# Hybrid decoder trunk: a sum of squares as a row product, a scan's products one piece later, and a second state buffer in linear attention

## The chip, the cores and the metric

The kernel runs on one core of a Trainium2 chip. The metric is the device time of one execution in microseconds (us). The kernel before took 2375.83 us (median of three runs, 2368.9 to 2376.44).

The core's engines have short names in the views: PE (TensorE's matmuls) and PEld (its weight loads), DVE (VectorE), ACT (ScalarE), POOL (GpSimd) and SP (SyncE, which here only issues DMAs). Each engine works through its own queue in order. DMAs are issued from SP's and from ACT's queue.

## What is computed

One layer of a decoder over 2048 tokens and 16 learned meta tokens, width 1024. A combined projection of the normed input feeds two branches: a Mamba-2 state-space branch (16 heads in 4 groups) and gated linear attention (4 heads). The branches are gated, projected, merged, projected once more and normed. The change touches two places of it, cut here to what matters:

```python
# state-space branch: after the scan, an RMS norm over each group's 256 channels
y = jnp.concatenate([y_m, y_r], axis=1) + d_skip[:, None] * xs
y = y.reshape(b, l, D_SSD) * jax.nn.silu(z)
y_ssd = rmsnorm(y.reshape(b, l, SSD_GROUPS, D_SSD // SSD_GROUPS),
                ssd_norm_w.reshape(SSD_GROUPS, -1)).reshape(b, l, D_SSD)

# linear attention: the state that goes from chunk to chunk
def step(s, inp):
    qi, ki, vi, gi = inp
    o_inter = jnp.einsum('bhtk,bhkv->bhtv', qi * jnp.exp(gi), s)
    ...
    g_last = gi[:, :, -1]
    k_dec = ki * jnp.exp(g_last[:, :, None, :] - gi)
    s_new = jnp.exp(g_last)[..., None] * s + jnp.einsum('bhsk,bhsv->bhkv', k_dec, vi)
    return s_new, o_inter + o_intra
```

## The kernel before

**Tiling and stages.** The tokens are worked through in four blocks of 512 (the first also holds the 16 meta tokens). In a block, features lie on the 128 partitions and tokens along the free dimension. Most products are split: each fp32 operand is cut into a high and a low part (fp32r), and `accum` (L187) makes three matmuls of them, high by high, high by low, low by high. A projection of one tile of 128 features (`proj_feat`, L193) is 8 x 3 = 24 matmuls with 512 columns. After the four blocks comes a second stage with the gates, the branch products and the output product, which the change doesn't touch.

**The order of the work.** The main loop (L850 to L860) runs over blocks, and in each block over 4 state-space groups (`ssd_proj`, L475) and 4 attention heads (`gla_proj`, L675). Both are generators. From one yield to the next they emit one projection; this is called a *piece* here. A state-space group has 6 pieces: four feature tiles (two of x, one each of B and C), then two tiles of the gate z. Group 0 has two more ahead of them, for the first values and the time steps. After each piece `step()` (L835) moves every running side generator on to its next yield, the oldest first. Such generators are the scan of a group (`ssd_scan`, begun at the fourth feature tile, L501), the scan of a head (`gla_scan`, begun after the keys, L644), the gates' logarithms (`gates`, L428), the loading of the next block's input (`fetch_u`), and `make_sums` (L73), which loads pieces of earlier results through SP, subtracts them on POOL (L81) and stores them through ACT's queue (L84). For PE and SP the order in which the program emits instructions is the order in which they run (the manual schedule of L849). For DVE, ACT and POOL a scheduler decides the order when the program is built, with its own estimate of times.

**Accesses and buffers.** The framework puts in the semaphores. Tiles come from pools with a number of buffers per tag: "act" (pairs of feature tiles, 4), "tok4" (6), "sq" (5), "gg" (4), "c1" (6), and for PSUM "pj" and "pt" (3 banks each) and "pc" (2 banks). A new tile waits until a buffer of its tag is free.

**The state-space scan** (`ssd_scan`, L518). Its first part fetches a row of cumulated decays (`fetch_cb`) and the factors `yf` by DMA. The part after the next yield makes the first products on PE: the scores of all four chunks (L551), then transposes of the first chunk (L565); they read the feature tiles that ACT (L497) and DVE (L498) finish. Then come four chunks of 128 tokens, one a part. The tail adds the skip term and multiplies by the gate (L613, L615), squares on ACT (L616) and adds the two tiles (L617) into `zs[0]`. One piece later PE sums over the channels: four matmuls (L621) with a strided quarter of `zs[0]` as the stationary operand and a column of ones as the moving one give the sums of 512 tokens as a [128, 4] tile. `rstd_of` (L230) takes the reciprocal root: DVE (L232), then POOL (L233). The result goes to DRAM (L623) and comes back broadcast over the partitions (L625). Two pieces later L630 on DVE multiplies and L631 stores the branch's result.

**The attention scan** (`gla_scan`, L685). After seven levels of products between halves of chunks (L734) and the assembly of the scores, the four chunks are done two to a piece. In each chunk one PSUM bank `po` takes two products: `po[:, 256:]` the state's increment (three matmuls on `kdt`), `po[:, :256]` the output (three on `atp`, and then L808, query times old state, in fp32). DVE then makes the new state in place:

```python
accum(po[:, 256:], [t[:, c] for t in kdt], vc, True, True)
accum(po[:, :256], [t[:, c] for t in atp], vc, True, False)
nc.tensor.matmul(po[:, :256], q[:, c * P:(c + 1) * P], s_gla[:, h], start=False, stop=True)
nc.vector.scalar_tensor_tensor(s_gla[:, h], s_gla[:, h], egl[:, c:c + 1], po[:, 256:],
                               op0=ALU.mult, op1=ALU.add)
```

These are L806 to L810. L811 and L813 on ACT copy the output out of `po` and square it.

**Other names.** `dt_chain` (L377) computes the time steps of a block; its results `tkd`, `tkc`, `wde`, `dec` have two buffers each (L365), and it uses scratch tiles `de`, `dw`, `dl`. The row of 512 sums or roots per group goes through small DRAM tiles (L368).

Of the kernel before, what the change touches and what calls it, by code (L numbers as in the profile page):

```python
# [7 lines left out]
F32 = mybir.dt.float32  # L8
# [6 lines left out]
P = 128  # L15
# [10 lines left out]
NSQ = 5  # L26
NT4 = 6
NACT = 4
NC1 = 6
LEVELS = (1, 2, 4, 8, 16, 32, 64)  # L30
NMSK = len(LEVELS)
# [10 lines left out]
def trunk_kernel(ctx: ExitStack, tc: tile.TileContext, xm, xmt, w_feat, w_tok, w_vm, w_br, w_o,  # L42
# [311 lines left out]
    def new_block(b, u):  # L354
        o = Block()
        o.b, o.u = b, u
        o.m0 = META if b == 0 else 0
        o.tt = o.m0 + BLK
        o.segs_all = [(0, o.tt // 2), (o.tt // 2, o.tt // 2)] if b == 0 else [(0, BLK)]
        o.segs_real = [(o.m0, BLK)]  # L360
        o.starts = [o.m0 + c * P for c in range(NCH)]
        o.chunks = ([(0, META)] if o.m0 else []) + [(a, P) for a in o.starts]
        o.ci0 = 1 if o.m0 else 0
        o.nck = len(o.chunks)
        for nm in ("tkd", "tkc", "wde", "dec"):  # L365
            setattr(o, nm, mk(bpool, [P, 5, NH], F32, nm, bufs=2))
        o.cumd = mk(dpool, [NH, BLK], F32, "cumd")
        o.ecud = mk(dpool, [NH, BLK], F32, "ecud")  # L368
        o.rstd = [mk(dpool, [P, NCH], F32, f"rstd{g}") for g in range(SG)]
        o.g_all = mk(bpool, [P, GH, META + BLK], F32, "g_all")  # L370
        o.gla = {}
        o.alr = mk(bpool, [P, 5, 48], F32, "alr")
        o.mov = lambda kt, a, n: tuple(t[:, kt, a:a + n] for t in u)
        return o


    def dt_chain(o, psd):  # L377
        m0, nck, ci0 = o.m0, o.nck, o.ci0
        tkd, tkc, wde, dec = o.tkd, o.tkc, o.wde, o.dec

        def t80(tag):
            return mk(sm, [P, 5, NH], F32, tag, bufs=1)[:, :nck]

        x = t80("dx")
        for i in range(nck):
            nc.vector.tensor_tensor(x[:, i], psd[i][:, 256:272], hv[:, 0], op=ALU.add)
            nc.scalar.activation(
                o.alr[:, i].rearrange("p (r c) -> p r c", c=16),
                psd[i][:, 272:288].unsqueeze(1).to_broadcast([P, 3, 16]), AF.Copy)
        e = t80("de")  # L390
        nc.scalar.activation(e, x, AF.Abs)
        nc.scalar.activation(e, e, AF.Exp, scale=-1.0)
        w1 = t80("dw")
        nc.vector.tensor_scalar(w1, e, 1.0, None, op0=ALU.add)
        ln = t80("dl")
        nc.scalar.activation(ln, w1, AF.Ln)
        nc.vector.scalar_tensor_tensor(e, w1, 1.0, e, op0=ALU.subtract, op1=ALU.subtract)
        nc.vector.tensor_tensor(ln, ln, e, op=ALU.subtract)
        dt = tkd[:, :nck]
        nc.vector.scalar_tensor_tensor(dt, x, 0.0, ln, op0=ALU.max, op1=ALU.add)  # L400
        nc.vector.tensor_tensor(x, dt, nega.unsqueeze(1).to_broadcast([P, nck, NH]), op=ALU.mult)
        yield
        ps = bank(pt, "pt")
        nc.tensor.matmul(ps[:, :nck * NH], tri, x.rearrange("p c h -> p (c h)"), start=True, stop=True)
        nc.vector.tensor_copy(tkc[:, :nck].rearrange("p c h -> p (c h)"), ps[:, :nck * NH])
        ps = bank(pt, "pt")
        if m0:
            nc.tensor.matmul(ps[:, :NH], ones[:META], x[:META, 0], start=True, stop=True)
        nc.tensor.matmul(ps[:, ci0 * NH:nck * NH], ones, x[:, ci0:].rearrange("p c h -> p (c h)"),
                         start=True, stop=True)  # L410
        psv = ps[:, :nck * NH].rearrange("p (c h) -> p c h", h=NH)
        nc.scalar.activation(dec[:, :nck], psv, AF.Exp)
        nc.vector.tensor_tensor(wde[:, :nck], psv, tkc[:, :nck], op=ALU.subtract)
        nc.vector.tensor_scalar(wde[:, :nck], wde[:, :nck], 0.0, None, op0=ALU.min)
        nc.scalar.activation(wde[:, :nck], wde[:, :nck], AF.Exp)
        nc.vector.tensor_tensor(wde[:, :nck], wde[:, :nck], dt, op=ALU.mult)
        yield
        ps = bank(pt, "pt")
        for c in range(NCH):
            nc.tensor.transpose(ps[:NH, c * P:(c + 1) * P], tkc[:, ci0 + c], ident)  # L420
        cr = mk(wk, [P, 3 + META + BLK], F32, "cin")[:NH, :BLK]
        nc.scalar.activation(cr, ps[:NH], AF.Copy)
        nc.scalar.dma_start(o.cumd, cr)
        er = mk(wk, [P, 3 + META + BLK], F32, "cin")[:NH, :BLK]
        nc.scalar.activation(er, ps[:NH], AF.Exp)
        nc.scalar.dma_start(o.ecud, er)
# [48 lines left out]
    def ssd_proj(o, g):  # L475
        m0, tt = o.m0, o.tt
        feats, zs = [], []
        if g == 0:
            yield from first_values(o)
        for j in range(4):  # L480
            ti = g * 4 + j
            pss = proj_feat(f"s{ti}", w_feat[T_SSD + ti], o.segs_all, o.mov)
            cin = mk(wk, [P, 3 + META + BLK], F32, "cin")
            acc = mk(wk, [P, META + BLK], F32, "acc")[:, :tt]
            nc.scalar.activation(cin[:, 0:3], tails[:, ti, :], AF.Copy)
            for ps, (a, n) in zip(pss, o.segs_all):
                nc.scalar.activation(cin[:, 3 + a:3 + a + n], ps[:, :n], AF.Copy)
                nc.scalar.activation(acc[:, a:a + n], ps[:, :n], AF.Identity, scale=hcw[:, ti, 3:4],  # L488
                                     bias=hcb[:, ti:ti + 1])
            nc.gpsimd.tensor_copy(tails[:, ti, :], cin[:, tt:tt + 3])  # L490
            for k in range(3):
                nc.vector.scalar_tensor_tensor(acc, cin[:, k:k + tt], hcw[:, ti, k:k + 1], acc,  # L492
                                               op0=ALU.mult, op1=ALU.add)
            if j % 2 == 0:
                two = pair_tile()
            f = two[:, j % 2]
            nc.scalar.activation(f[:, :tt], acc, AF.Tanh)  # L497
            nc.vector.scalar_tensor_tensor(f[:, :tt], f[:, :tt], 1.0, acc, op0=ALU.add, op1=ALU.mult)  # L498
            feats.append(f)
            if j == 3:  # L500
                begin(ssd_scan(o, g, feats, zs))  # L501
            yield
        for j in range(2):
            ti = 2 * g + j
            ps, = proj_feat(f"z{ti}", w_feat[T_Z + ti], o.segs_real, o.mov)
            zt = mk(wk, [P, BLK], F32, "gg", bufs=4)
            nc.scalar.activation(zt, ps, AF.Tanh, scale=0.5)
            nc.vector.scalar_tensor_tensor(zt, zt, 1.0, ps, op0=ALU.add, op1=ALU.mult)
            zs.append(zt)
            yield  # L510
# [7 lines left out]
    def ssd_scan(o, g, feats, zs):  # L518
# [4 lines left out]
        yf = mk(wk, [P, NCH, 256], F32, "tok4", bufs=NT4).rearrange("p c f -> p (c f)").rearrange("p (j t) -> p j t", j=2)  # L523
        for i in range(2):
            nc.scalar.dma_start(yf[64 * i:64 * i + 64], o.ecud[4 * g + i:4 * g + i + 3:2, :].unsqueeze(0).to_broadcast([64, 2, BLK]))
        yield
        hs = slice(4 * g, 4 * g + 4)

# [87 lines left out]
            nc.scalar.activation(zs[j], yf[:, j], AF.Square)  # L616
        nc.vector.tensor_tensor(zs[0], zs[0], zs[1], op=ALU.add)  # L617
        yield
        ps = bank(pt, "pt")
        for c in range(NCH):  # L620
            nc.tensor.matmul(ps[:, c:c + 1], zs[0][:, c::NCH], ones[:, :1], start=True, stop=True)  # L621
        r = rstd_of(ps[:, :NCH], NCH, 1.0 / 1024)
        nc.scalar.dma_start(o.rstd[g], r)  # L623
        rb = mk(wk, [P, BLK], F32, "gg", bufs=4)
        nc.scalar.dma_start(rb, o.rstd[g].rearrange("p c -> (p c)").unsqueeze(0).to_broadcast([P, BLK]))  # L625
        yield
        yield
# [37 lines left out]
    def gla_out_gates(o, h):  # L665
        t0 = T_GLA + 4 * h
        for j in range(2):
            ps, = proj_feat(f"g{t0 + 2 + j}", w_feat[t0 + 2 + j], o.segs_real, o.mov)
            gg = mk(wk, [P, BLK], F32, "gg", bufs=4)
            nc.scalar.activation(gg, ps, AF.Tanh, scale=0.5)  # L670
            nc.vector.scalar_tensor_tensor(gg, gg, 1.0, ps, op0=ALU.add, op1=ALU.mult)
            o.gla[h][1].append(gg)
            yield
# [11 lines left out]
    def gla_scan(o, h, kq, vals, gs):  # L685
# [111 lines left out]
        split(*[t[:, 2:] for t in atp], ps[:, :256].rearrange("p (c t) -> p c t", t=P))  # L797
        yield

        vt = vals[0]  # L800
        ot = mk(wk, [P, NCH, 256], F32, "ot", bufs=1)
        ssq = mk(sm, [P, 4], F32, "ssq")
        for c in range(NCH):
# [1 line left out]
            vc = [t[:, c] for t in vt]  # L805
            accum(po[:, 256:], [t[:, c] for t in kdt], vc, True, True)  # L806
            accum(po[:, :256], [t[:, c] for t in atp], vc, True, False)
            nc.tensor.matmul(po[:, :256], q[:, c * P:(c + 1) * P], s_gla[:, h], start=False, stop=True)  # L808
            nc.vector.scalar_tensor_tensor(s_gla[:, h], s_gla[:, h], egl[:, c:c + 1], po[:, 256:],
                                           op0=ALU.mult, op1=ALU.add)  # L810
            nc.scalar.activation(ot[:, c], po[:, :256], AF.Copy)  # L811
            jk = mk(wk, [P, 256], BF16, "junk", bufs=1)
            nc.scalar.activation(jk, po[:, :256], AF.Square, accum_out=ssq[:, c:c + 1])  # L813
# [426 lines left out]
```

## Time and profile before

| | us |
|---|---|
| median of three runs | 2375.83 |
| lowest and highest | 2368.9, 2376.44 |
| the profiled execution | 2377.53 |
| its span, first to last instruction | 2375.7 |
| blocks 0 to 3 with both branches, in the span | 0 to about 1577 |
| second stage, in the span | about 1577 to 2375.7 |

The mean granted TensorE clock of the profiled execution was 0.979 of the full one. PE's busy time by the windows of the profile was 244.6 us of the first 272 us, 174.1 of the next 178 (up to 450), and 775.3 of the 798.7 us of the second stage.

How to read it: the views name a group of instructions by its line in the kernel, its engine, its operation and its tiles (out<-in, with the buffer numbers left out). `L189` to `L191` are the three matmuls of `accum`; the tiles tell which product it is. `L237` and `L238` are the two halves of `split`. A wait is idle time of an engine ahead of an instruction, with the instruction or the DMA that ended it. An idle engine costs time only where PE later waits for it.

### The profile page before, as it was taken

The page shows a single profiled execution, that of the slowest core. Times are in us where ns is not written, and L with a number is a line of the kernel's source. Part 1 is how long each engine was busy: PE and PEld are TensorE (multiplying, and loading weights), DVE is VectorE, ACT ScalarE, POOL GpSimd, SP SyncE. Part 2 cuts the span into 40 slices and gives each one's busy share as a digit, 9 for nine tenths or more (in the row PEclk, how much of TensorE's full clock was granted, in tenths as well). Part 3 has the DMA queues.
Part 4 walks back from the last instruction along what each step waited for, and adds up shares of the span by engine and source line. Part 5 has one row for each costly group of instructions (what it writes and reads, how often), then busy time and mean ns, then how long its engine had stood idle before and what let it go on. Part 6 is the DMA issues. An engine that isn't in the chain of part 4 may idle for free.

```text
span 2375.7 us, 34516 instructions
## 1 busy us (share of the span) xinstructions
PE 2270.2 (96%) x12009; PEld 1925.5 (81%) x12009; DVE 1445.9 (61%) x2467; ACT 1091.8 (46%) x2390; POOL 679.7 (29%) x681
## 2 busy tenths in 40 slices
PE   7999999999999999999999999979999999999998
PEld 6888888877888887888887789867888888888776
DVE  5676664466654456555356554455578854778776
ACT  4655554454433354433345333354545454554443
POOL 4343432212211112221112200027433355424231
PEclk9999999999999999999999999989999999999999
DMA  8776875777776677786587754457667876687743
GB/s 294 250 233 226 268 244 187 224 220 238 243 257 184 206 238 226 222 269 214 179 246 214 226 165 155 142 166 246 208 243 262 285 243 213 237 278 262 249 147 125
DMA packets 310877, 530.66 MB, mean 223 GB/s; under 512 B 30832, under 2 KB 146800, under 8 KB 310704
## 3 DMA queue, kind: packets, MB, share of 16 engines
q1 hardware_dynamic: 200400, 402.84, 52.6%
q10 hardware_dynamic: 110304, 125.63, 16.5%
q8 instruction: 94, 1.54, 0.3%
q14 instruction: 79, 0.65, 0.1%
HBM read 381.00 MB, written 147.36 MB: 222 GB/s over the span
## 4 chain that ended last, share of the span: by engine, by line
PE 71%; DMA 11%; DVE 6%; issue 4%; ACT 4%; POOL 2%; SPq 1%; ACTq 1%; POOLq 0%; DVEq 0%
PE pj L189 16%; PE pj L191 16%; PE pj L190 16%; PE pt L189 3%; PE pt L191 3%; PE pt L190 3%; PE pt L734 2%; DVE acc L492 2%; PE pc L190 2%; PE pc L189 2%; PE pc L191 2%; POOL wr L81 2%; DMA gg<-rstd 2%; DMA wr<-y 1%; PE pc L590 1%
## 5 line engine op out<-in xcount | busy, mean ns | idle before, releaser
L189 PE MATMUL pj<-u,whl 128*128 128x512 f32 (+1 forms) x1440 | 554.5, 385 | 6.1 <-ACT acc L488 3.9
L191 PE MATMUL pj<-u,whl 128*128 128x512 f32 (+1 forms) x1440 | 533.4, 370 | 0.8 <-POOL whl L170 0.8
L190 PE MATMUL pj<-u,whl 128*128 128x512 f32 (+1 forms) x1440 | 533.1, 370 | 0.0
L189 PEld LDWEIGHTS pj<-u,whl 128*128 128x128 f32 x1440 | 275.9, 192 | 52.5 <-ACT acc L488 5.6
L191 PEld LDWEIGHTS pj<-u,whl 128*128 128x128 f32 x1440 | 274.3, 190 | 47.7 <-POOL whl L170 1.1
L190 PEld LDWEIGHTS pj<-u,whl 128*128 128x128 f32 x1440 | 275.7, 191 | 42.4
L189 PE MATMUL pj<-b,a 128*128 128x512 f32 x640 | 254.5, 398 | 10.1 <-ACT sn L952 8.0
L190 PE MATMUL pj<-b,a 128*128 128x512 f32 x640 | 252.1, 394 | 1.8 <-DVE b L911 1.8
L191 PE MATMUL pj<-b,a 128*128 128x512 f32 x640 | 252.6, 395 | 0.0
L170 POOL TENSOR_TENSOR whl<-wr,whl 128x512 fp32r<-128x512 f32 (+1 forms) x100 | 133.4, 1339 | 191.1 <-ACT whl L169 168.5
L911 DVE TENSOR_TENSOR b<-br,b 128x512 fp32r<-128x512 f32 x196 | 152.7, 799 | 47.7 <-ACT b L910 45.2
L492 DVE SCALAR_TENSOR_TENSOR acc<-cin,hcw,acc 128x512 f32<-128x512 f32 (+1 forms) x192 | 159.9, 833 | 34.3 <-ACT acc L488 33.1
L926 POOL TENSOR_TENSOR as<-ar,ar 128x512 f32<-128x512 f32 x40 | 60.5, 1512 | 409.1 <-DMA ar<-in_w_br 151.0
L910 ACT ACTIVATE b<-br 128x512 fp32r<-128x512 f32 x196 | 119.2, 626 | 103.6 <-DMA br<-br_t 32.3
L936 DVE TENSOR_TENSOR a<-ar,a 128x512 fp32r<-128x512 f32 x160 | 126.8, 800 | 65.6 <-ACT a L935 63.5
L81 POOL TENSOR_TENSOR wr<-wr 128x256 f32<-128x256 f32 x80 | 69.0, 862 | 338.1 <-DMA wr<-y 142.6
L189 PEld LDWEIGHTS pj<-b,a 128*128 128x128 f32 x640 | 121.5, 190 | 38.5 <-ACT sn L952 10.2
L189 PE MATMUL pj<-whl,u 128*128 128x256 f32 (+1 forms) x480 | 143.7, 299 | 2.9 <-ACT u L307 1.5
L190 PEld LDWEIGHTS pj<-b,a 128*128 128x128 f32 x640 | 121.6, 190 | 29.0 <-DVE b L911 2.2
L191 PEld LDWEIGHTS pj<-b,a 128*128 128x128 f32 x640 | 121.5, 190 | 27.7
L191 PE MATMUL pj<-whl,u 128*128 128x256 f32 (+1 forms) x480 | 140.0, 292 | 1.4 <-DVE u L309 1.4
L190 PE MATMUL pj<-whl,u 128*128 128x256 f32 (+1 forms) x480 | 139.7, 291 | 0.0
(270 smaller groups left out, 4738.2 us busy)
## 6 DMA issues: line engine op xcount, KB each, us to landing
whl<-k_s SPq DMA_DIRECT2D x96, 512.0 KB, 4.5
whl<-k_g SPq DMA_DIRECT2D x96, 512.0 KB, 4.3
whl<-k_z SPq DMA_DIRECT2D x48, 512.0 KB, 3.7
wr<-in_w_feat SPq DMA_DIRECT2D x80, 256.0 KB, 4.2
whl<-k_v SPq DMA_DIRECT2D x36, 512.0 KB, 3.8
k_s<-whl SPq DMA_DIRECT2D x32, 512.0 KB, 3.5
cb<-cumd ACTq DMA_DIRECT2D x64, 256.0 KB, 5.4
k_g<-whl SPq DMA_DIRECT2D x32, 512.0 KB, 3.8
```

The costliest lines, as they stand in the source:

```text
L81: nc.gpsimd.tensor_tensor(o, x, y, op=ALU.subtract)
L170: nc.gpsimd.tensor_tensor(hl[:, 1], raw, hl[:, 0].bitcast(F32), op=ALU.subtract)
L189: nc.tensor.matmul(ps, sh, mh, start=first, stop=False, **kw)
L190: nc.tensor.matmul(ps, sh, ml, start=False, stop=False, **kw)
L191: nc.tensor.matmul(ps, sl, mh, start=False, stop=last, **kw)
L492: nc.vector.scalar_tensor_tensor(acc, cin[:, k:k + tt], hcw[:, ti, k:k + 1], acc, op0=ALU.mult, op1=ALU.add)
L590: nc.tensor.matmul(py[:, (2 + j) * P:(3 + j) * P], s_ssd[:, g, j * P:(j + 1) * P], cf[:, a:a + P], start=True, stop=True)
L734: nc.tensor.matmul(ps[:, r * P:(r + 1) * P], packed[0][:, r * P:(r + 1) * P], odd_even(half, m0 + (r + 2) * P, P // (2 * half), k_to_q - 2 ...
L910: nc.scalar.activation(t[:, 0], raw, AF.Copy)
L911: nc.vector.tensor_tensor(t[:, 1], raw, t[:, 0].bitcast(F32), op=ALU.subtract)
L926: nc.gpsimd.tensor_tensor(s1, a21, a22, op=ALU.add)
L936: nc.vector.tensor_tensor(t[:, 1], src, t[:, 0].bitcast(F32), op=ALU.subtract)
```

## The change

The diff, without the lines that only replace a number by a name:

```diff
+NGG = 5
...
         for nm in ("tkd", "tkc", "wde", "dec"):
-            setattr(o, nm, mk(bpool, [P, 5, NH], F32, nm, bufs=2))
+            setattr(o, nm, mk(bpool, [P, 5, NH], F32, nm))
...
+        o.ssq = [mk(dpool, [P, NCH], F32, f"ssq{g}") for g in range(SG)]
...
-        e = t80("de")
+        e = wde[:, :nck]
...
-        w1 = t80("dw")
+        w1 = tkc[:, :nck]
...
-        ln = t80("dl")
+        ln = dec[:, :nck]
...
             nc.scalar.dma_start(yf[64 * i:64 * i + 64], o.ecud[...])
         yield
+        yield
         hs = slice(4 * g, 4 * g + 4)
...
         nc.vector.tensor_tensor(zs[0], zs[0], zs[1], op=ALU.add)
         yield
+        sqh, sql = [mk(wk, [P, BLK], F32R, "sq", bufs=NSQ) for _ in range(2)]
+        nc.scalar.activation(sqh, zs[0], AF.Copy)
+        nc.gpsimd.tensor_tensor(sql, zs[0], sqh.bitcast(F32), op=ALU.subtract)
+        yield
         ps = bank(pt, "pt")
-        for c in range(NCH):
-            nc.tensor.matmul(ps[:, c:c + 1], zs[0][:, c::NCH], ones[:, :1], start=True, stop=True)
-        r = rstd_of(ps[:, :NCH], NCH, 1.0 / 1024)
+        for i, t in enumerate((sqh, sql)):
+            nc.tensor.matmul(ps[:1], ones_r[:, :1], t, start=i == 0, stop=i == 1)
+        rb = mk(wk, [P, BLK], F32, "gg", bufs=NGG)
+        nc.scalar.activation(rb[:1], ps[:1], AF.Copy)
+        nc.scalar.dma_start(o.ssq[g].rearrange("p c -> (p c)").unsqueeze(0), rb[:1])
+        s4 = mk(sm, [P, NCH], F32, "ssq")
+        nc.scalar.dma_start(s4, o.ssq[g])
+        yield
+        r = rstd_of(s4, NCH, 1.0 / 1024)
         nc.scalar.dma_start(o.rstd[g], r)
-        rb = mk(wk, [P, BLK], F32, "gg", bufs=4)
         nc.scalar.dma_start(rb, o.rstd[g].rearrange("p c -> (p c)").unsqueeze(0).to_broadcast([P, BLK]))
...
-        vt = vals[0]
+        vt, s_in = vals[0], s_gla[:, h]
...
-            nc.tensor.matmul(po[:, :256], q[:, c * P:(c + 1) * P], s_gla[:, h], start=False, stop=True)
-            nc.vector.scalar_tensor_tensor(s_gla[:, h], s_gla[:, h], egl[:, c:c + 1], po[:, 256:],
-                                           op0=ALU.mult, op1=ALU.add)
+            s_out = s_gla[:, h] if c % 2 else mk(wk, [P, 256], F32, "c1", bufs=NC1)
+            nc.vector.scalar_tensor_tensor(s_out, s_in, egl[:, c:c + 1], po[:, 256:], op0=ALU.mult, op1=ALU.add)
+            nc.tensor.matmul(po[:, :256], q[:, c * P:(c + 1) * P], s_in, start=False, stop=True)
+            s_in = s_out
```

The parts in words:

- The tail of the state-space scan cuts its summed squares into a high part (ACT) and a low part (POOL), a piece later makes the sum as a row with two matmuls (a column of ones stationary, 512 tokens moving), copies the row out of PSUM, sends it to DRAM and reads it back as [128, 4], and a piece after that takes the root as before. These are two yields more.
- One more yield after the scan's first part moves all the rest of the scan one piece later. The last step of a scan so comes three pieces later than before.
- In the attention scan the first chunk of a piece writes its new state into a "c1" buffer, the second chunk writes it back to `s_gla`. The state's update is emitted ahead of the product of the query and the old state.
- "gg" has five buffers instead of four. `tkd`, `tkc`, `wde` and `dec` have one buffer instead of two, and three of them also serve as scratch in place of `de`, `dw` and `dl`.

More of the change, by code (lines that the diff above doesn't have):

```diff
@@ L505, in ssd_proj @@
             ps, = proj_feat(f"z{ti}", w_feat[T_Z + ti], o.segs_real, o.mov)
-            zt = mk(wk, [P, BLK], F32, "gg", bufs=4)
+            zt = mk(wk, [P, BLK], F32, "gg", bufs=NGG)
             nc.scalar.activation(zt, ps, AF.Tanh, scale=0.5)
@@ L668, in gla_out_gates @@
             ps, = proj_feat(f"g{t0 + 2 + j}", w_feat[t0 + 2 + j], o.segs_real, o.mov)
-            gg = mk(wk, [P, BLK], F32, "gg", bufs=4)
+            gg = mk(wk, [P, BLK], F32, "gg", bufs=NGG)
             nc.scalar.activation(gg, ps, AF.Tanh, scale=0.5)
```

## The prediction

> **What bounds the kernel now.** I read the busy row and the chain of the page, then the view of waits, then the groups by line and short timelines around the lines that the change touches.
>
> ```profile
> span 2375.7 us, 34516 instructions
> PE 2270.2 (96%) x12009; PEld 1925.5 (81%) x12009; DVE 1445.9 (61%) x2467; ACT 1091.8 (46%) x2390; POOL 679.7 (29%) x681
> PE 71%; DMA 11%; DVE 6%; issue 4%; ACT 4%; POOL 2%; SPq 1%; ACTq 1%; POOLq 0%; DVEq 0%
> ```
>
> TensorE (PE) is the bound: it is idle for 2375.7 - 2270.2 = 105.5 us, and its order is written out by hand, so a matmul that waits holds up all that stand behind it. Time can change in three ways only: PE gets less work, a PE wait goes, or a PE wait appears. Work on the other engines costs nothing until PE waits for it. So the waits come next.
>
> ```profile
> POOL wr L81 <- DMA wr<-y: 143.0, 19, 22.0
> ...
> DVE tok L630 <- DMA gg<-rstd: 58.5, 16, 6.1
> ...
> ACT ot L811 <- DVE s_gla L809: 39.3, 48, 1.3
> ...
> DVE s_gla L809 <- PE pc L808: 33.2, 32, 5.6
> ...
> PE pc L808 <- DVE s_gla L809: 16.6, 10, 2.5
> ...
> PE pc L551 <- DVE act L498: 11.0, 7, 2.5
> PE pt L621 <- DVE gg L617: 10.7, 6, 3.5
> ```
>
> The columns are total us, times, longest us. The last three rows are PE's own and each belongs to one part of the change: the attention state (L808), the scan's first products (L551), the sum of squares (L621). The other rows matter for what is queued where.
>
> **The row product.** Each of the 16 scans has four fp32 matmuls of one column, which the trace shows as eight instructions.
>
> ```profile
> L621 PE MATMUL pt<-ones_r,gg 128*128 128x1 f32 x128 | 30.3, 358 | 10.7 <-DVE gg L617 10.7
> ...
> L779 PE MATMUL pt<-sq,ones_r 128*128 128x512 f32 x32 | 11.8, 453 | 0.0
> ```
>
> ```profile
> 615.23 1.80 PE L621 MATMUL pt<-ones_r,gg 128*128 128x1 f32 x8
> 616.89 1.14 PE L551 MATMUL pc<-act 128*128 128x128 f32 x8
> ```
>
> From the first of the eight to the next work is 616.89 - 615.23 = 1.66 us. The new form, two matmuls of 512 columns with a stationary of ones, stands in this kernel already: L779, 16 pairs. The groups give the difference: 30.3 - 11.8 = 18.5 us less PE work. The 10.7 us of waiting before L621 goes as well, since the products are emitted two pieces behind the addition L617 instead of one, and a piece is a projection of 24 matmuls, some 9 us (24 x 370 ns). The new ACT copy and POOL subtraction fit into that piece, by these rows of the same shapes:
>
> ```profile
> L237 ACT ACTIVATE sq<-sq 128x512 fp32r<-128x512 f32 x16 | 10.0, 622 | 8.2 <-DVE tok L630 8.1 <-DVE c L742 0.2
> ...
> L170 POOL TENSOR_TENSOR whl<-wr,whl 128x512 fp32r<-128x512 f32 (+1 forms) x100 | 133.4, 1339 | 191.1 <-ACT whl L169 168.5 <-PE pt L757 6.5 <-PE pt L191 6.1
> ```
>
> That is 0.62 + 1.34 = 1.96 us of 9. If the cover is gone (POOL stuck behind L81, third rival), PE pays.
>
> **The scan's first products a piece later.** The 11.0 us of L551 waiting for the feature tiles (L498) goes, since they get 9 us more and the longest wait is 2.5 us. The scan now spans 12 pieces instead of 9 before its last step. What that holds longer: yf (6 "tok4" buffers: at most three yf and two values at once in the SSD groups), the feature pairs (4 "act" buffers: in group 1, with the gates' own pair, the third feature tile waits a piece longer for its buffer, and its products also come a piece later, so the slack stays), the "sq" buffers (two halves, one mask, two decay tiles: all five) and the "gg" buffers (five, so the fifth is needed). I cost all of these at nothing; the cover is the added piece, and without it they are L551 waits again, 11.0 us at most. The single buffers of tkd, tkc, wde, dec, and their use as scratch, cost nothing: the next block writes them 20 pieces after the last scan read them.
>
> **The two added DMAs.** The sum goes to DRAM as a row and comes back as four columns, both on ACT's queue, before L232. Their nearest rows are those of the reciprocal root:
>
> ```profile
> L623 ACTq DMA_DIRECT2D rstd<-rstd x16: 322/336/344, 138.7 to 1423.3; - x16
> L625 ACTq DMA_DIRECT2D gg<-rstd x16: 326/338/357, 142.6 to 1424.8; - x16
> ...
> DMA to landing us min/median/max: 1.4/4.8/7.0
> ```
>
> So ACT issues 2 x 0.34 us more a scan and its queue stands for up to a landing (4.8 us) at the second DMA, which waits for the first; behind it stand the PSUM evictions of the projection. L232 on VectorE (DVE) now waits for a landing too; DVE already stands 58.5 / 16 = 3.7 us at L630 for the same reason. PE's share of such standing cannot be read off directly. Lower bound 0 (everything that stands catches up before PE needs it), upper bound 16 us, one us for each of the 16 scans, about a quarter of DVE's existing 3.7 us. I take 6 us, nearer the lower end, since PE waits for an eviction (ACT acc L488) are a few us in the whole of the existing kernel:
>
> ```profile
> L189 PE MATMUL pj<-u,whl 128*128 128x512 f32 (+1 forms) x1440 | 554.5, 385 | 6.1 <-ACT acc L488 3.9
> ```
>
> Scan part: -18.5 - 10.7 - 11.0 + 6 = -34 us. Bounds: -40 (nothing given back) and -20 (14 us more given back: 10 us of the 21.7 us of waits reappear behind busy DVE and ACT, and 10 us of standing).
>
> **The second state buffer.** It frees the update L809 from the read of the old state by L808. But the update is now also emitted ahead of L808, and both use one PSUM bank: `po[:, 256:]` is read, `po[:, :256]` is written. The trace shows what a shared bank means here. L811 reads only `po[:, :256]`, L809 only `po[:, 256:]`; they share no data, yet ACT waited for L809 48 times of 64 (39.3 us, above). A clean pair of chunks, PE, then DVE, then ACT:
>
> ```profile
> 361.14 0.28 PE L191 MATMUL pc<-tok,atp 128*128 128x256 f32 x1
> 361.25 0.59 PE L808 MATMUL pc<-s_gla,act 128*128 128x256 f32 x2
> ...
> 362.27 0.28 PE L191 MATMUL pc<-tok,atp 128*128 128x256 f32 x1
> 362.51 0.70 PE L808 MATMUL pc<-s_gla,act 128*128 128x256 f32 x2
> ```
>
> ```profile
> 361.98 0.47 DVE L809 SCALAR_TENSOR_TENSOR s_gla<-s_gla,egl,pc 128x256 f32<-128x256 f32 x1
> 363.25 0.48 DVE L809 SCALAR_TENSOR_TENSOR s_gla<-s_gla,egl,pc 128x256 f32<-128x256 f32 x1 [0.79 <-PE pc L808]
> ```
>
> ```profile
> 362.49 0.38 ACT L811 ACTIVATE ot<-pc 128x256 f32<-128x256 f32 x1 [0.63 <-DVE s_gla L809]
> 363.76 0.38 ACT L811 ACTIVATE ot<-pc 128x256 f32<-128x256 f32 x1 [0.53 <-DVE s_gla L809]
> ```
>
> L808 of the second chunk ended at 362.51 + 0.70 = 363.21; both L809 and L811 could have started, L809 ran 363.25 to 363.73, and L811 began only at 363.76. So accesses to one bank by two engines are put in program order, even reads of different halves. A write by PE after a read by DVE will be too. The Trainium skill, "PSUM — Partial Sum Buffer", section "PSUM bank collisions raise a hardware error", gives this rule: two engines at one bank and the same partitions at once collide, disjoint columns included, so the order must be guarded by bank and not by address. By that rule the wait below appears, without it the first rival comes out; the ACT rows agree, and no run here yet shows a PE write held up by a DVE read.
>
> New order in one chunk: six matmuls, then L809, then L808. From the rows: the sixth ends at 361.14 + 0.28 = 361.42; L809 starts 0.04 later (363.21 to 363.25), takes 0.48, and PE follows 0.06 after it (361.98 + 0.47 = 362.45, L808 at 362.51). L808 starts at 362.00 instead of 361.25: 0.75 us, in each of 64 chunks: 48 us. Before, only the second chunk of a pair could wait, and most of its wait lay beside its own six matmuls.
>
> The 16.6 us of existing waits come from DVE being busy or itself waiting when L809 is due:
>
> ```profile
> 742.71 2.15 ACTq L84 DMA_DIRECT2D gate_t<-wr  x2
> 744.96 0.60 ACT L670 ACTIVATE gg<-pj 128x512 f32<-128x512 f32 x1 [6.46 <-POOL wr L81]
> ```
>
> ```profile
> 745.59 0.69 DVE L671 SCALAR_TENSOR_TENSOR gg<-gg,pj 128x512 f32<-128x512 f32 x1 [7.55 <-ACT gg L670]
> 746.19 0.47 DVE L809 SCALAR_TENSOR_TENSOR s_gla<-s_gla,egl,pc 128x256 f32<-128x256 f32 x1
> ```
>
> Here L809 stands behind L671, that behind ACT, that behind a store that waits for POOL. None of this is removed; it moves to the first chunk of the pair. The 48 us come on top, less some 3 us of small waits that they contain. DVE was not waiting for PE ahead of 32 of the 64 updates (the row with 32 times), so these can be late by part of an instruction, until now unseen by PE in every second chunk: 0 to 32 x 0.4 = 13 us. I take 5. Sum +50 us; bounds +29 (all 16.6 us vanish) and +58 (all 13 appear). Behind the waiting L808 on PE stand the next projection and the other heads' products; nothing else profits from the pause.
>
> **Sum.** -34 + 50 = +16 us on the profiled execution, 2377.5 us (span 2375.7 and 1.8 around it): 2393.5. The median of the runs shown, 2375.8, is 1.7 lower, so 2392. Ends: -40 + 29 = -11 (2365) and -20 + 58 = +38 (2414).
>
> **Rivals.**
> 1. Faster: the bank doesn't bind. If L809 is released by the third of the six matmuls and L808 doesn't wait for its own chunk's L809, the second buffer does what it says: the update has 0.75 us more cover, and most of the 16.6 us goes with the scan's 34: -50 us, 2326. It decides at L808 in each first chunk. Against it: L811's 39.3 us. Chance 8%.
> 2. No change: the two halves cancel. The scan gives its full 40 us and the state costs 33 to 47: within 7 us of 2376. About 0.3%, 7 us, is what a measurement of this kernel can tell from no change. For it: both sums are close and of opposite sign. Chance 20%. A further 7%: slightly faster than that, at the -11 end.
> 3. Slower still: the subtraction on POOL stands behind L81, which waits for its loads (143.0 us, up to 22.0). If PE then waits some 3 us in half of the 12 scans of blocks 1 to 3, and the standing DMAs cost the full 16 us: +16 + 18 + 10 = +44, 2420. Against: a whole piece of reserve and long idle stretches of POOL. Chance 7%.
>
> **How the numbers follow.** The forecast, slower by 7 to 38 us, has 58%. Slower is 58 + 7 = 65%, same 20%, faster 8 + 7 = 15%. The range from 2365 to 2414 is the two ends of the sum; it leaves out rivals 1 and 3, 15%.
>
> **What would show it.** In the changed profile: PE waits of L808 for L809 rise from 16.6 us in 10 to some 57 us in about 64 (right; of each 0.75 us the view shows 0.04 + 0.48 + 0.06 = 0.58 as idle: 37 us, with 16.6 and a few), or fall below 10 us (rival 1). L809 follows a PE matmul of `accum` and no longer L808; ACT's wait for L809 disappears. The row product costs about 12 us of PE; waits of its first matmul and of L551's successor are near zero (a wait for POOL there is rival 3). DVE stands at the root's first step for a DMA, 2 to 5 us a scan. The forecast is wrong if PE's idle time does not rise, or if the linear attention's stages do not get longer by about 12 us a block.

## The result, and the profile after

The changed kernel took 2469.94 us (median of four runs) against 2372.36 us of the kernel before beside it: a ratio of 1.041, 95% interval 1.037 to 1.045. It is slower by some 98 us, where +16 was forecast and +38 was the upper end. The profiled execution took 2473.0 us, with a span of 2470.9.

Each view below uses the line numbers of its own run's kernel. The page of the changed kernel, the rows that answer to those of before:

```profile
span 2470.9 us, 34456 instructions
PE 2287.4 (93%) x11913; PEld 1922.5 (78%) x11913; DVE 1446.2 (59%) x2467; ACT 1103.8 (45%) x2422; POOL 700.5 (28%) x697
PE 53%; DMA 17%; issue 10%; DVE 8%; ACT 7%; POOL 3%; SPq 1%; ACTq 1%; POOLq 0%; DVEq 0%
```

PE's idle time rose from 105.5 us to 2470.9 - 2287.4 = 183.5 us. PE's share of the chain fell from 71% to 53%, and DMA and issue took its place. One number doesn't fit a story of waits alone: PE has 96 instructions fewer, the row product is shorter, and yet PE is busy for 17 us *longer*.

By stretches (from the first feature projection of a block, for the first block from the start of the span, to its first key projection, and on to the next block), in us:

| | before | after |
|---|---|---|
| state-space groups, four blocks | 800.5 | 822.1 |
| attention heads, four blocks | 781.2 | 856.8 |
| second stage | 794.1 | 792.0 |

So attention lost 75.6 us where 50 were forecast, and the state-space groups lost 21.6 where 34 were to be won. The view of waits of the changed kernel, the rows that count (L821 is the state's update, L822 the product with the old state, L590 the scan's product, before L587):

```profile
ACT ot L824 <- PE pc L822: 78.9, 50, 2.5
...
DVE tok L642 <- DMA gg<-rstd: 48.5, 15, 6.4
...
PE pc L822 <- DVE c L821: 42.3, 32, 3.8
...
DVE rstd L233 <- DMA ssq<-ssq: 37.3, 13, 5.6
...
PE pc L590 <- DVE s_ssd L599: 25.6, 12, 3.8
...
PE pc L822 <- DVE s_gla L821: 21.5, 32, 2.1
...
PE pj L190 <- ACT g_all L453: 14.0, 4, 4.3
...
PE pt L808 <- DVE sq L796: 9.5, 3, 4.5
```

What the forecast named is there: PE waits for the update of its own chunk in 64 chunks of 64, 42.3 + 21.5 = 63.8 us (57 was expected), and ACT's wait for L809 is gone, replaced by one for PE. The waits at the sum of squares are gone too. What it did not name is the rest of the list: L590, L453 and L808, together 49.1 us, none of them in PE's list of before at this size.

A pair of chunks in the changed kernel, PE and then DVE, to be laid beside the pair shown in the prediction:

```profile
373.39 0.28 PE L192 MATMUL pc<-tok,atp 128*128 128x256 f32 x1
374.25 0.70 PE L822 MATMUL pc<-c,act 128*128 128x256 f32 x2 [0.57 <-DVE s_gla L821]
```

```profile
373.71 0.48 DVE L821 SCALAR_TENSOR_TENSOR s_gla<-c,egl,pc 128x256 f32<-128x256 f32 x1 [1.50 <-PE pc L192]
```

The sixth matmul ends at 373.67, L821 starts 0.04 us later and ends at 374.19, L822 starts at 374.25: 0.86 us after the sixth matmul began, where the clean step of before was 0.11 (361.14 to 361.25). That is the 0.75 us of the forecast, to the hundredth.

### The profile page after: what moved, and what is told of

Its sections match the earlier page's. It is cut to its first block, busy times and chain, and to the rows that moved or that the text cites. A ratio compares the mean times of both kernels' runs of the same rounds, so it can differ in the third digit from the quotient of the medians.

```text
span 2470.9 us, 34456 instructions
## 1 busy us (share of the span) xinstructions
PE 2287.4 (93%) x11913; PEld 1922.5 (78%) x11913; DVE 1446.2 (59%) x2467; ACT 1103.8 (45%) x2422; POOL 700.5 (28%) x697
## 4 chain that ended last, share of the span: by engine, by line
PE 53%; DMA 17%; issue 10%; DVE 8%; ACT 7%; POOL 3%; SPq 1%; ACTq 1%; POOLq 0%; DVEq 0%
PE pj L190 12%; PE pj L192 12%; PE pj L191 12%; PE pt L190 3%; PE pt L192 3%; PE pt L191 3%; DMA gg<-rstd 2%; DMA acc<-in_xm 2%; DMA rstd<-rstd 2%; DMA wr<-u 2%; DVE acc L494 2%; POOL wr L82 2%; PE pc L822 1%; PE pc L192 1%; PE pc L191 1%
## 5 line engine op out<-in xcount | busy, mean ns | idle before, releaser
L190 PE MATMUL pj<-u,whl 128*128 128x512 f32 (+1 forms) x1440 | 565.1, 392 | 25.6 <-ACT g_all L453 14.0
L192 PE MATMUL pj<-u,whl 128*128 128x512 f32 (+1 forms) x1440 | 541.9, 376 | 0.8 <-POOL whl L171 0.8
L191 PE MATMUL pj<-u,whl 128*128 128x512 f32 (+1 forms) x1440 | 542.3, 377 | 0.0
L190 PEld LDWEIGHTS pj<-u,whl 128*128 128x128 f32 x1440 | 282.6, 196 | 75.7 <-ACT g_all L453 15.6
L192 PEld LDWEIGHTS pj<-u,whl 128*128 128x128 f32 x1440 | 280.2, 195 | 49.4 <-POOL whl L171 1.0
L191 PEld LDWEIGHTS pj<-u,whl 128*128 128x128 f32 x1440 | 281.9, 196 | 44.4
L190 PE MATMUL pj<-whl,u 128*128 128x256 f32 (+1 forms) x480 | 141.4, 295 | 3.4 <-DMA whl<-k_vm 1.9
L192 PE MATMUL pj<-whl,u 128*128 128x256 f32 (+1 forms) x480 | 138.0, 288 | 1.5 <-DVE u L310 1.5
L191 PE MATMUL pj<-whl,u 128*128 128x256 f32 (+1 forms) x480 | 137.7, 287 | 0.0
```

Source lines behind the costliest of these rows:

```text
L190: nc.tensor.matmul(ps, sh, mh, start=first, stop=False, **kw)
L191: nc.tensor.matmul(ps, sh, ml, start=False, stop=False, **kw)
L192: nc.tensor.matmul(ps, sl, mh, start=False, stop=last, **kw)
```

## The experiments

Two theories stood at the start. The first: two separate costs, the shared PSUM bank in attention (some 75 us) and late DVE and ACT in the state-space scan (some 22 us). The rival: the scan's part is the gain that was forecast, and attention's stalls alone brought the other waits with them.

**One part at a time.** The changed kernel with the attention loop of before:

```diff
...
-            nc.vector.scalar_tensor_tensor(s_out, s_in, egl[:, c:c + 1], po[:, 256:], ...)
-            nc.tensor.matmul(po[:, :256], q[...], s_in, start=False, stop=True)
...
+            nc.tensor.matmul(po[:, :256], q[...], s_gla[:, h], start=False, stop=True)
+            nc.vector.scalar_tensor_tensor(s_gla[:, h], s_gla[:, h], egl[:, c:c + 1], po[:, 256:], ...)
```

> The changed kernel with the attention loop of before; the scan's part, its buffers and its DMAs stay. Theory (two separate costs: the shared PSUM bank in attention, some 75 us by the stages' lengths, and late DVE and ACT in the scan, some 22 us): 2385 to 2400 us, with L590 and L453 waits still there. Rival (the scan's part is a gain of some 34 us as forecast, and the attention's stalls alone made the later scan waits): 2335 to 2350 us.

Measured: 2392.0 us against 2373.0, ratio 1.008 (1.005 to 1.011). The scan's part loses 19 us by itself, and the waits named are there: 23.3 us at L590 and 13.1 us at L453. The rival falls.

The kernel before with only the attention loop of the change:

> The kernel before with the attention loop of the change alone (second buffer, update emitted ahead of the product). Theory: 64 stalls of 0.75 us and more, and half-clock windows behind them: 2435 to 2455 us. Rival (the stalls are only moved, and cost little alone): within 15 us of 2372.

Measured: 2446.5 us, ratio 1.029 (1.025 to 1.033), some 73 us above before. Its page and its waits:

```profile
PE 2301.4 (94%) x12009; PEld 1943.4 (79%) x12009; DVE 1453.9 (59%) x2467; ACT 1092.3 (45%) x2390; POOL 680.7 (28%) x681
```

```profile
PE pc L810 <- DVE c L809: 44.1, 32, 3.3
...
PE pc L810 <- DVE s_gla L809: 19.8, 32, 1.4
```

Same instructions as before (12009), idle time 2447.1 - 2301.4 = 145.7, so 40 us more than before; busy time 31 us more. Of these 31, some 10 are the matmul in front of each stall, whose end no longer overlaps a successor (64 x (0.28 - 0.12) = 10, an estimate). The other 20 us or so are put down to matmuls that ran slower: the mean granted clock was 0.970, against 0.979 before; see the clock below.

**Buffer, order or bank.** The second buffer, but the product emitted ahead of the update as before (against the kernel before):

```diff
-            nc.tensor.matmul(po[:, :256], q[...], s_gla[:, h], start=False, stop=True)
-            nc.vector.scalar_tensor_tensor(s_gla[:, h], s_gla[:, h], egl[:, c:c + 1], po[:, 256:], ...)
+            s_out = s_gla[:, h] if c % 2 else mk(wk, [P, 256], F32, "c1", bufs=NC1)
+            nc.tensor.matmul(po[:, :256], q[...], s_in, start=False, stop=True)
+            nc.vector.scalar_tensor_tensor(s_out, s_in, egl[:, c:c + 1], po[:, 256:], ...)
+            s_in = s_out
```

> The kernel before with the second buffer for the state, but the product emitted ahead of the update as before. Theory (the order in the bank costs, the buffer doesn't): 2365 to 2378 us, L809 waits as before. Rival (the extra c1 buffer in use, or its placing, costs): 2400 us or more.

Measured: 2373.9 us, ratio 1.000 (0.997 to 1.002). PE's waits for the update are 15.0 us in 12, much as before. The buffer costs nothing and brings nothing in the old order.

The order of the change, but the increment in a bank of its own (against the run of the attention loop alone):

```diff
             po = bank(pc, "pc")
+            pk = bank(pt, "pt")
-            accum(po[:, 256:], [t[:, c] for t in kdt], vc, True, True)
+            accum(pk[:, :256], [t[:, c] for t in kdt], vc, True, True)
...
-            nc.vector.scalar_tensor_tensor(s_out, s_in, egl[:, c:c + 1], po[:, 256:], ...)
+            nc.vector.scalar_tensor_tensor(s_out, s_in, egl[:, c:c + 1], pk[:, :256], ...)
             nc.tensor.matmul(po[:, :256], q[...], s_in, start=False, stop=True)
```

> As the attention loop of the change, on the kernel before, but the state's increment goes into a PSUM bank of its own (from pt). Theory (the bank binds, not the data): the wait of the query product for its own chunk's update goes, 2350 to 2375 us. Rival (the cost is in the order of emission itself, whatever the bank): 2430 us or more, as the state alone.

Measured: 2354.3 us, ratio 0.990 (0.985 to 0.995). PE in the same pair of chunks, and the wait that is left:

```profile
363.20 0.28 PE L191 MATMUL pc<-tok,atp 128*128 128x256 f32 x1
363.31 0.59 PE L811 MATMUL pc<-s_gla,act 128*128 128x256 f32 x2
...
364.33 0.28 PE L191 MATMUL pc<-tok,atp 128*128 128x256 f32 x1
364.45 0.60 PE L811 MATMUL pc<-c,act 128*128 128x256 f32 x2
```

```profile
PE pc L811 <- DVE c L810: 6.3, 5, 1.7
```

L811 starts 0.11 us after the sixth matmul: no stall. Order and buffer are those of the change, only the bank differs: 2446.5 falls to 2354.3. Sharing the bank is the cause of the loss. (Each bank is one tile in this kernel, so an order kept by bank and one kept by tile look the same here.) Without it the time is some 19 us below before. How much of these 19 is the new order with its buffer, and how much the bank alone, is not shown: ACT's waits for the update (39.3 us before) are gone too, and no run has the own bank with the old order.

**What is wrong in the scan.** Theory A: the shift by a piece puts the scan's DVE work into the wrong pieces. Theory B: the added DMA trip makes DVE and ACT stand. The extra yield alone, on the kernel before:

```diff
         yield
+        yield
         hs = slice(4 * g, 4 * g + 4)
```

> The kernel before with the one extra yield after the scan's first part and nothing else. Theory A (the shift puts the four chunks' work on DVE into the pieces that hold the four convolutions, and the tail into the gates' pieces, so L587, the scan's own product, waits for a PSUM bank that DVE still reads): the 11 us of L551 go, some 15 to 25 us of L587 and gates' waits come, 2375 to 2390 us. Theory B (the added DMA trip makes DVE and ACT late; the shift is harmless): 2360 to 2368 us, L551's waits gone and no new ones.

Measured: 2367.9 us, ratio 0.997 (0.995 to 0.999): a gain of 5 us, at the upper end of B's range. The 11.0 us of L551 are gone, as both say, and the 10.7 us at the sum of squares too; but 12.9 + 7.7 = 20.6 us of A's waits came:

```profile
PE pj L189 <- ACT g_all L451: 12.9, 4, 4.3
...
PE pj L448 <- ACT act L439: 7.7, 4, 3.1
```

The tail (L613 to L617 before, one line further down here) now falls into the piece in which the gates need DVE and ACT, and the gates' bank is one that the projections need. In this run's trace DVE makes the tail's L614 and L616 between 904.47 and 907.75, shortly ahead of the gates' L450 at 908.26, and PE waits 3.91 us for what follows from L450. Neither theory alone gives this run.

The row product with its two DMAs and the buffers of the change, but without that yield:

> The changed kernel without the extra yield after the scan's first part and with the attention loop of before: row product, its two DMAs and the buffers only. Theory A: a gain from the 18.5 us of PE work and the 10.7 us of waits that stays, 2345 to 2360 us. Theory B: DVE and ACT stand at the DMA trip and PE waits for them, 2380 us or more.

Measured: 2417.1 us, ratio 1.017 (1.014 to 1.020): 44 us lost by the part that was to win most. Its waits:

```profile
DVE tok L641 <- DMA gg<-rstd: 52.5, 16, 5.9
...
DVE rstd L233 <- DMA ssq<-ssq: 45.3, 13, 6.9
...
PE pc L553 <- DVE act L500: 38.3, 13, 4.5
...
PE pc L589 <- DVE tok L601: 12.6, 5, 5.1
...
PE pc L589 <- DVE s_ssd L598: 10.7, 5, 4.5
```

The DMA trip, on the four strided matmuls of before (the buffers are those of the change, and the root comes one piece later):

```diff
-        r = rstd_of(ps[:, :NCH], NCH, 1.0 / 1024)
+        s3 = mk(sm, [P, NCH], F32, "ssq")
+        nc.scalar.activation(s3, ps[:, :NCH], AF.Copy)
+        nc.scalar.dma_start(o.ssq[g], s3)
+        s4 = mk(sm, [P, NCH], F32, "ssq")
+        nc.scalar.dma_start(s4, o.ssq[g])
+        yield
+        r = rstd_of(s4, NCH, 1.0 / 1024)
```

> The kernel before with the four strided matmuls kept, but their [128, 4] sums sent to DRAM and read back ahead of the root, one piece earlier than the root, as in the change: the DMA trip by itself, with the change's buffers. Theory B: 2385 to 2395 us. Theory A: 2370 to 2380 us.

Measured: 2391.4 us against 2373.2, ratio 1.007 (1.005 to 1.010). With these buffers the trip costs 18 us; theory B's number. Two rows of PE's waits grew most:

```profile
PE pj L190 <- ACT acc L490: 9.0, 6, 3.9
...
PE pc L589 <- DVE s_ssd L598: 5.8, 4, 2.4
```

The first was 3.9 us before; the second was not in PE's list. How landings get to PE is read best in chains of the changed kernel, in order of time (start, us, what). The first runs through the added trip, the root and the two old DMAs to an attention head's score tile, which DVE finishes at L796 behind L642:

```profile
1126.13 2.25 DMA ssq<-ssq
...
1130.24 6.45 DMA rstd<-rstd
...
1136.77 5.59 DMA gg<-rstd
...
1143.05 0.74 DVE tok L642
...
1144.40 0.65 DVE sq L796
...
1145.18 0.41 PE pt L808 x2
```

PE had waited 4.5 us by then. The second:

```profile
582.38 3.79 DMA rstd<-rstd
...
586.19 4.17 DMA gg<-rstd
...
590.38 1.43 DVE tok L642 x2
...
592.21 0.60 ACT cin L489
592.80 0.68 ACT acc L490
...
594.59 0.34 DVE s_ssd L599
...
594.97 0.66 PE pc L590 x8
```

Two landings follow each other. DVE stands at L642 for the second one, ACT stands behind the store of L642's result before it can evict the next projection (L489), and the state's update L599, whose bank L590 needs, comes after both. PE had waited 3.62 us by then. The two DMAs of this chain stood in the kernel before as well; the trip adds two more landings and a second place for DVE to stand, L233 (37.3 us).

The same row product without any of the four small DMAs: all 128 columns of ones as the stationary operand put the sum on every partition, and ACT makes the root as exp(-0.5 ln x). The cut shows it against the row product of the change; the buffers are those of the kernel before.

```diff
-            nc.tensor.matmul(ps[:1], ones_r[:, :1], t, start=i == 0, stop=i == 1)
+            nc.tensor.matmul(ps, ones_r, t, start=i == 0, stop=i == 1)
...
+        nc.scalar.activation(rb, ps, AF.Ln, scale=1.0 / 1024, bias=eps_c)
+        nc.scalar.activation(rb, rb, AF.Exp, scale=-0.5)
+        yield
```

> The kernel before with the row product, but with 128 columns of ones as the stationary operand, so that the sum stands on all partitions at once; the root is made by ACT (logarithm and exponential), and none of the four small DMAs of the tail is left. No extra yield at the scan's start. Theory B (DVE and ACT standing at small DMAs is the price): clearly below the row alone, 2325 to 2345 us, and DVE's 58.5 us at L630 gone. Theory A: as the row alone within 8 us.

Measured: 2368.9 us, ratio 0.999 (0.997 to 1.001). This is 48 us below the row product with DMAs. The two runs also differ in the buffers, in the root's engine and in when the last step comes (two pieces), so the 48 us are not the DMAs' alone beyond doubt; but the waits point to them: DVE's 45.3 and 52.5 us at landings are gone, and PE's waits at L589 fall from 23.3 to 2.5 us. Still it misses both expectations: PE has some 20 us less work in the sum of squares than before (30.3 to 9.9), none of the four DMAs is left, and the time is that of before. The first products tell why. Before and this run:

```profile
L551 PE MATMUL pc<-act 128*128 128x128 f32 x128 | 22.3, 329 | 11.0 <-DVE act L498 11.0
```

```profile
L553 PE MATMUL pc<-act 128*128 128x128 f32 x128 | 22.8, 334 | 35.8 <-DVE act L500 35.8
```

In the order of before, L621 stands just ahead of L551 in the same step. While PE did the slow sum and waited for it, the feature tiles became ready. With the sum gone from there (it comes a piece later), PE comes to L551 sooner and waits there for the same tiles: 24.8 us more. The traces bear this out: in the second block's third group the last tile was ready 3.93 us after the projection's last matmul began, and is 4.15 us after it here, but PE waited 0.90 us for it before and 3.91 here. The row product with DMAs shows the same wait, 38.3 us. The gain was handed on to the next wait. If so, the extra yield, worth 5 us alone, should now be worth much more:

> The row product on all partitions with the root on ACT and no small DMAs, and the one extra yield at the scan's start. Theory (behind L621's work and waits stood the late feature tiles: with L621 shorter, PE waits for the same DVE work at L551 instead, unless the yield gives it a piece more): the 36 us of L551 waits of the run without the yield go, 2335 to 2352 us. Rival (DVE is late by itself, the waits turn up at L587 and the gates): 2360 to 2370 us.

Measured: 2353.7 us against 2371.2, ratio 0.992 (0.991 to 0.994), a little above the range. The tiles' waits are gone:

```profile
L554 PE MATMUL pc<-act 128*128 128x128 f32 x128 | 16.9, 275 | 0.0
```

The yield is worth some 15 us here. The rival's waits (gates, 13.0 and 7.3 us in this run) stay, which is why it isn't more.

**Together.** The same with the attention state in its own bank:

> The same with the attention state's second buffer and a PSUM bank of its own for the increment. Theory (the two parts add): some 18 us below the run without the own bank, 2315 to 2340 us. Rival (the bank taken from pt is now missed by the scan): no more than 5 us below it.

Measured: 2335.0 us, ratio 0.985 (0.983 to 0.987): 36 us below before, 135 below the changed kernel, and the fastest of all. The parts add: 18.7 us below the run without the own bank, as much as the own bank brought alone.

```profile
PE 2241.8 (96%) x11913; PEld 1889.4 (81%) x11913; DVE 1455.5 (62%) x2452; ACT 1157.6 (50%) x2470; POOL 681.8 (29%) x681
```

And the changed kernel itself with nothing altered but the increment's bank:

> The whole changed kernel with one thing altered: the state's increment has a PSUM bank of its own. Theory (the shared bank is the attention part's whole cost, and the rest is the scan's): 2365 to 2385 us, the scan part alone less the own bank's gain of 18 us. Rival (the two parts make each other worse by more than the bank): 2395 us or more.

Measured: 2362.5 us against 2371.2, ratio 0.997 (0.995 to 0.998), slightly under the range. One bank turns the changed kernel from 98 us slower to 9 us faster, 107 us. Between the two runs of the attention part alone (2446.5 and 2354.3) it is 92 us. The intervals of the four ratios are too wide to tell whether the stalls and the late scan make each other worse.

## Why the prediction was wrong, point by point

Alone, the scan's part cost 19 us where a gain of 34 was forecast, and the state's part 73 us where 50 were. So most of the miss is the scan's: two waits counted as gains that were handed on, and landings priced too low. The rest is mostly a slower clock, which the forecast put at nothing.

- **The bound and the bank: right.** PE's order sets the time. The update in the shared bank holds PE up in all 64 chunks, by 0.75 us in the clean case, as worked out. The run with a bank of its own shows that it is the bank. The rule of the Trainium skill ("PSUM — Partial Sum Buffer", section "PSUM bank collisions raise a hardware error"), which no run had shown for a PE write, agrees now as to the order kept: a PE write to one half of a bank stood behind a DVE read of the other, 63.8 us in 64 waits. What happens without that order no run here shows.
- **The size of the state part: a term was missing.** The forecast had +50. In the run of that part alone idle time rose by 40 us and the matmuls' loose ends by 10, so the 50 us were right (with a little luck: PE's waits for the update rose by 47 us, and 7 us of other waits fell away). What failed is the silent step that PE works at the same speed behind a stall. Some 20 us came on top by a slower clock, behind the long stalls and not the regular ones (below).
- **The row product, -18.5 us: the work was right, the gain wrong.** The new group is L628, 10.0 us of PE, where 11.8 was assumed. But without the DMAs and the yield almost nothing of it reached the time (2368.9 against 2373.2).
- **The waits that go, -10.7 and -11.0 us: the step that failed.** Each went where it was named. They were counted as if independent, though L621 and L551 stand in one step of PE, one behind the other, and wait for work of the same two engines. Taking the slow sum and its wait from in front of L551 made that wait 24.8 us longer; the yield alone took both waits away, 21.7 us, and brought 5 us, because PE then waited 20.6 us for the gates.
- **The standing at DMAs, +6 us, at most 16: mis-sized.** The trip costs 18 us on the old sum, and in the row product without the yield the run without the four small DMAs is 48 us faster. The forecast took the few us of L488 waits as the measure. They did rise, by 5.1 us with the trip; the larger part in the row product turned up at L587 (L589 there), whose bank DVE must first leave: 23.3 us, against 2.5 without the DMAs.
- **"Cover" of the moved tail: wrong place looked at.** Buffers were counted. Not counted was which other work of DVE and ACT lies in the pieces to which the tail and the last step move: in group 1, behind the tail, the gates (14.0 us at L453), and behind the last step L642, which itself stands for landings, the attention head's score tile (9.5 us at L808). The cover is also smaller than the 9 us reckoned: 24 x 370 ns adds up matmuls that overlap. They start 0.23 us apart (598.11 to 598.34 in the trace of before), so that 24 take some 5.5 us.
- **Third rival** (the POOL subtraction late behind L81): didn't happen. No wait of PE for L624 shows in the changed kernel.

Open: how the 48 us divide between the two added and the two old small DMAs in the row product, since no run has one pair without the other, and what the buffers of the change cost by themselves, since no run has them alone. How much of the changed kernel's 98 us is clock rather than waits can be estimated from the traces: some 30 us, as the last section works out.

## What to carry to other kernels

Before an instruction of one engine is put between two of another, look whether they share a PSUM bank, not whether they share data: here a bank of its own was worth 107 us and decided whether the change lost or won. A wait removed from an in-order engine is a gain only as far as the next instruction isn't late for the same reason, so ask of each removed wait what the next one was waiting for meanwhile. And a round trip through DRAM off the critical path still stops the queues in which its readers stand: here one such trip in each of 16 scans, with the change's buffers, cost 18 us.

## What the runs showed of the hardware

**A long stall is paid twice.** PE behind a stall of 3.62 us in the changed kernel:

```profile
594.97 0.66 PE L590 MATMUL pc<-sq,c 128*64 128x128 f32 x8 [3.62 <-DVE s_ssd L599]
...
597.90 0.63 PE L192 MATMUL pj<-u,whl 128*128 128x512 f32 x1
598.32 0.63 PE L190 MATMUL pj<-u,whl 128*128 128x512 f32 x1
...
599.77 0.40 PE L191 MATMUL pj<-u,whl 128*128 128x512 f32 x1
600.00 0.40 PE L192 MATMUL pj<-u,whl 128*128 128x512 f32 x1
```

The step from one 512-column matmul to the next is 0.42 us up to about 599.4, then 0.23. The windows' view of the two stretches (PEclk is the third number from the end, the granted clock):

```profile
596.10:599.40 3.30, 3.30 (x10) 2.66 (x9) 2.57 (x4) 1.33 (x4) 1.85 (x3) 0.50 0.52 187
599.60:603.00 3.40, 3.40 (x17) 2.77 (x16) 2.91 (x5) 0.46 (x1) 0.61 (x2) 1.00 0.44 118
```

The granted clock was 0.50 and then 1.00. It fell about 1.1 us after PE had gone on at 594.97. The Trainium skill ("TensorE: Matmul & The Clock Gate", section "Part 1: The HAM clock gate (the "warmup" mystery)") says that an idle window of about 3.4 us brings half the clock until a busy one has passed. The trace agrees in the two levels, and a stretch of some 3.4 us at half clock stands behind this stall. It doesn't agree in how long PE must stand. In slices of half a microsecond, the changed kernel's trace has half clock behind each of the 25 PE waits of 2.05 us and more (after the first 20 us): it starts in the wait or within 2.6 us of its end and lasts 3.4 us or a multiple of that. Of the 74 waits between 0.5 and 1.75 us outside such stretches only 4 have one behind them, each within 2.5 us of a longer wait; of the 7 in between, 2 have. So the regular stalls at the shared bank, 1.1 us in a pair's first chunk and 0.57 us in its second, aren't followed by a slower clock; the 8 waits of L822 of over 2 us, for which DVE came late, are.

The mean granted clock went from 0.979 before to 0.966 after, and to 0.970 with the attention part alone. With two levels only, that is 2 x 0.021 x 2375.7 = 100 us at half clock before and 2 x 0.034 x 2470.9 = 168 us after. The 68 us more cost at most half of that, 34 us, by this estimate. PE's busy time shows the price: 2287.4 us in the changed kernel, 2245.5 with the same instructions and the state's increment in its own bank, 42 us of which about 10 are the loose ends in front of the stalls, so some 30 are clock:

```profile
PE 2245.5 (95%) x11913; PEld 1895.9 (80%) x11913; DVE 1451.2 (61%) x2467; ACT 1101.5 (47%) x2422; POOL 697.5 (30%) x697
```

So a wait of PE of more than some 2 us should be priced at its own length and, behind it, at up to 1.7 us more for each 3.4 us at half clock.

**A column of ones loads fast, but nothing is won by it.** L628's weight loads of one column took 83 ns each, against 188 for the 128 columns of the run without DMAs, and its matmuls 395 ns, against 392 there. The sum on all partitions costs PE the same as the sum on one.
